# Gathering and combining tokens for one expert at a time in a 64-expert mixture layer, with expert 0's down matrix in another pool

## The chip, the cores and the metric

The kernel runs on one core of one Trainium2 chip. The metric is the device time of one execution in microseconds (us). The names of the engines are those of the profile: PE is the matrix engine (TensorE), PEld its weight loads, DVE the vector engine, ACT the scalar engine, POOL GpSimd, and SP the queue that issues the large transfers. NT = 2 is the number of blocks of 128 tokens.

## The reference, cut to what matters

One decoder layer for 256 tokens of 2048 channels: a mixer, an output projection with a residual, a norm, and then a mixture of 64 experts of width 256, from which each token takes two, and a final norm. The change touches the mixture only.

```python
def hier_moe(x, w_group, b_group, w_router, b_router, w_gate, w_up, w_down):
    """Top-1 expert group, then top-2 experts within that group; SwiGLU experts."""
...
    out = jnp.zeros_like(xt)
    for g in range(N_GROUPS):
        h = jax.nn.silu(jnp.einsum('td,edf->tef', xt, wg[g])) * jnp.einsum('td,edf->tef', xt, wu[g])
        out = out + jnp.einsum('tef,efd->td', h * combine[:, g, :, None], wd[g])
```

All weights are float32. An expert has three matrices of 2 MB: gate (g), up (u) and down (d); below, d5 is the down matrix of expert 5.

## The kernel before

The mixer, the output projection and the routing take the time up to about 381 us. From there the kernel goes through the 64 experts in order. For each it needs a compact copy of the tokens that chose it (32 places, `SLOTS`), the expert's three matrices, and a place to add the result.

**Gather.** `gather(b)` does this for a batch of four experts (`EB`): one comparison makes a 0/1 matrix of 256 tokens by 4 x 32 places (tile `mo`), and 32 matrix products on the full array (`pxg`, L706) pick the tokens, already transposed, in four groups; DVE multiplies each group by the norm's gains into `XT` (L709). The gather of the next batch is called after the second expert of a batch.

**Expert.** `expert` multiplies gate and up (`pgu`, L757) on four column groups of the array, so that four channel blocks are in the PSUM tile under each other. ACT copies the tile (`gs`, L761), eight small products add the four blocks and transpose them (`pgt`, L766), ACT and DVE make silu(gate) * up (L770, L774), and `py` (L783) multiplies with the down matrix, again on four column groups.

**Combine.** The outputs of four experts are copied into four `Y` tiles, and `combine` multiplies them with the transposed combine weights of the batch (`poc`, L722, made by `places`) in 8 products on the full array, each added to the residual `h` by DVE (L805). The last four experts are combined alone: `combine_one` puts one 32-row strip on each of four row groups (L813), and DVE adds (L816).

**Loads.** `loads` issues one transfer for each matrix on SP, in order. Their homes are a ring of 8 tiles of 2 MB in four pools (`rings`), so the load of a matrix waits until PE has read the matrix eight places earlier in the ring. One matrix lies outside the ring: the down matrix of expert 1 goes into the two 8 KB-per-partition tiles (`half_acc`) that hold the residual later; the residual is put there by ACT (L1080) at expert 2. The pool `u8` has three tiles of 8 KB per partition: `mo` and two batches of `XT`.

**The rest.** `overflow` (tokens beyond 32 places, a branch that is not taken here) stands after expert 31. `gains` spreads the final norm's gains (`pgf`, L937) at expert 60. The last expert adds its output into the final norm's pass (`plast`). Tile framework and engine queues run each engine in program order, as placed by the scheduler.

Of the kernel before, what the change touches and what calls it, by code (L numbers as in the profile page):

```python
# [8 lines left out]
F32 = mybir.dt.float32  # L9
# [29 lines left out]
def hymba_kernel(ctx: ExitStack, tc, x, xt, norm_mix_g, w_in, w_gk, gla_norm_g, swa_sinks, w_out, norm_ffn_g, ffn_g_route, w_route,  # L39
# [649 lines left out]
    mo = u8([P, 2, 4, 256], "mo")  # L689
    hn = [0]  # L690

    XT, OC, Y4 = {}, {}, {}


    def gather(b):
        w4 = mo[:, b % 2].rearrange("p a b -> p (a b)")
        oh = w4[:, 0:NT * P].rearrange("p (t e s) -> p t e s", t=NT, e=EB)
        e0 = b * EB
        V.tensor_tensor(oh, iosl[:, None, None, :].to_broadcast([P, NT, EB, SLOTS]),  # L699
                        pos[:, :, e0:e0 + EB, None].to_broadcast([P, NT, EB, SLOTS]), op=OP.is_equal)  # L700
        XT[b] = u8([P, KT, P], f"XT{b}")
        for kg in range(4):
            p = ptmp(f"pxg{b}_{kg}")
            for j in range(4):
                for t in range(NT):
                    TE.matmul(p[:, j * P:(j + 1) * P], hgp[:, t, kg * 4 + j, :],  # L706
                              oh[:, t].rearrange("p e s -> p (e s)"), start=(t == 0), stop=(t == NT - 1))
            k4 = slice(kg * 4, kg * 4 + 4)
            V.tensor_tensor(XT[b][:, k4, :], p.rearrange("p (k i) -> p k i", k=4),  # L709
                            gT[:, k4, None].to_broadcast([P, 4, P]), op=OP.mult)  # L710
            yield


    def places(half, e0, n=EB):
        w4 = mo[:, half % 2].rearrange("p a b -> p (a b)")
        oc = w4[:, 256:256 + NT * P].rearrange("p (t e s) -> p t e s", t=NT, e=EB)
        V.tensor_tensor(oc, iosl[:, None, None, :].to_broadcast([P, NT, EB, SLOTS]),
                        pos[:, :, e0:e0 + n, None].to_broadcast([P, NT, EB, SLOTS]), op=OP.is_equal)
        V.tensor_tensor(oc, oc, Cs[:, :, e0:e0 + n, None].to_broadcast([P, NT, EB, SLOTS]), op=OP.mult)
        p = ptmp(f"poc{e0}")  # L720
# [437 lines left out]
```

## Time and profile before

| what | value |
|---|---|
| time, 3 runs | 1317.43 us median (1314.42 to 1317.8) |
| the profiled execution | 1319.65 us, span 1317.9 us |
| mean granted TensorE clock | 0.922 |
| PE busy | 1119.5 us (85%) |
| DVE busy | 482.9 us (37%) |
| ACT busy | 338.3 us (26%) |
| moved from HBM | 462.70 MB |

The span is the time from the first to the last instruction of the profiled execution; 1.75 us of its time lie outside. Each share is an average over stages: the mixture begins at about 381 us. A granted clock of 1 is full speed (2.4 GHz), of 0.5 half (1.2 GHz). The columns of a timeline row are start, duration, engine, line, operation, result and operands, shape, count and, in brackets, the engine's idle time before it and what ended it.

### The profile page before, as it was taken

The numbers are of one execution on the slowest core, as the hardware profiler recorded it, in microseconds if no ns is written. First come the engines' busy times: TensorE is split into PE (matmuls) and PEld (weight loads), VectorE is DVE, ScalarE is ACT, GpSimd is POOL, SyncE is SP. The second block draws the span as 40 slices with busy tenths as digits, with TensorE's granted clock in tenths as the row PEclk, the third lists the DMA queues.
The fourth block names the chain that finished last, engine by engine and source line by source line (L and its number), as shares of the span: only waits on it lengthen the run. The fifth ranks groups of instructions, "written<-read, shape, count | busy, mean of one in ns | idle before, by whom it ended". The sixth has DMA issues, their size and how long they took to land. (4 is left out here: it accounts for less than half of the span.)

```text
span 1317.9 us, 20950 instructions
## 1 busy us (share of the span) xinstructions
PE 1119.5 (85%) x9167; PEld 713.3 (54%) x9167; DVE 482.9 (37%) x833; ACT 338.3 (26%) x618; POOL 51.9 (4%) x107
## 2 busy tenths in 40 slices
PE   8999999999988987878787887788787787878786
PEld 8988778768875544434353534355353434435332
DVE  5666654455443432222322222223222222323224
ACT  7355554433434111111111111011111111111113
POOL 2120100020100000000000000000000000000002
PEclk9999999999999999888897989799798978889789
DMA  9735335557379999999999999999999999999993
GB/s 348 266 127 192 128 112 195 205 175 273 128 277 429 429 428 429 429 428 430 430 429 429 429 430 419 427 430 430 430 427 429 429 429 430 430 430 430 429 425 151
DMA packets 69391, 466.21 MB, mean 354 GB/s; under 512 B 4700, under 2 KB 25228, under 8 KB 43953
## 3 DMA queue, kind: packets, MB, share of 16 engines
q1 hardware_dynamic: 69058, 464.72, 85.4%
q8 instruction: 73, 1.20, 0.4%
q0 software_dynamic: 240, 0.14, 0.2%
q14 instruction: 20, 0.16, 0.0%
HBM read 462.70 MB, written 2.36 MB: 353 GB/s over the span
## 5 line engine op out<-in xcount | busy, mean ns | idle before, releaser
L757 PE MATMUL pgu<-w,XT 128*32 128x256 f32 x4096 | 266.3, 410 | 77.5 <-DMA w<-in_w_up_dram 47.5
L757 PEld LDWEIGHTS pgu<-w,XT 128*32 128x32 f32 x4096 | 132.9, 117 | 221.9 <-DMA w<-in_w_up_dram 64.1
L783 PE MATMUL py<-w,mo 128*32 128x512 f32 x1008 | 148.7, 715 | 33.5 <-DVE mo L774 17.9
L795 DVE COPY Y<-py 32x512 f32<-32x512 f32 x120 | 82.8, 690 | 191.0 <-ACT Y L797 190.2
L761 ACT ACTIVATE gs<-pgu 128x512 f32<-128x512 f32 x64 | 38.2, 597 | 410.9 <-PE pgu L757 410.7
L774 DVE TENSOR_TENSOR mo<-mo,pgt 128x64 f32<-128x64 f32 x63 | 13.9, 221 | 352.0 <-ACT mo L770 352.0
L803 PE MATMUL pc<-Y,mo 128*128 128x512 f32 x240 | 127.6, 692 | 10.0 <-ACT Y L797 10.0
L797 ACT ACTIVATE Y<-py 32x512 f32<-32x512 f32 x120 | 70.4, 587 | 253.4 <-PE py L783 208.3
L706 PEld LDWEIGHTS pxg<-mo,hgp 128*128 128x128 f32 x1024 | 118.2, 194 | 14.4 <-issue 14.4
L706 PE MATMUL pxg<-mo,hgp 128*128 128x128 f32 x1024 | 124.0, 280 | 0.9 <-DVE mo L699 0.9
L766 PE MATMUL pgt<-id,gs 128*128 128x32 f32 x512 | 73.4, 289 | 48.2 <-ACT gs L761 48.2
L766 PEld LDWEIGHTS pgt<-id,gs 128*128 128x128 f32 x512 | 66.1, 202 | 81.8 <-ACT gs L761 81.8
L803 PEld LDWEIGHTS pc<-Y,mo 128*128 128x128 f32 x240 | 51.8, 224 | 95.3 <-issue 50.3
L805 DVE TENSOR_TENSOR h<-h,pc 128x512 f32<-128x512 f32 x120 | 81.6, 687 | 35.8 <-PE pc L803 35.6
L783 PEld LDWEIGHTS py<-w,mo 128*32 128x32 f32 x1008 | 30.3, 119 | 87.8 <-issue 45.5
L709 DVE TENSOR_TENSOR XT<-pxg,gT 128x512 f32<-128x512 f32 x64 | 44.2, 692 | 60.4 <-PE pxg L706 60.3
L982 POOL IOTA fin<- 128x4 f32 x1 | 0.2, 158 | 899.5 <-DMA w<-in_w_up_dram 899.5
L770 ACT ACTIVATE mo<-pgt 128x64 f32<-128x64 f32 x64 | 14.3, 223 | 78.2 <-PE pgt L766 78.2
L154 PE MATMUL pt<-xh,wi0s 128*128 128x256 f32 x120 | 23.1, 287 | 1.8 <-ACT wi0s L148 1.1
L129 PE MATMUL pjr<-wir_0s,xh 128*128 128x512 f32 x64 | 21.5, 416 | 0.0
L154 PEld LDWEIGHTS pt<-xh,wi0s 128*128 128x128 f32 x120 | 19.0, 191 | 2.5 <-ACT wi0s L148 1.3
L129 PE MATMUL pjr<-wir_1s,xh 128*128 128x512 f32 x64 | 19.9, 391 | 0.0
(392 smaller groups left out, 1395.1 us busy)
## 6 DMA issues: line engine op xcount, KB each, us to landing
w<-in_w_up_dram SPq DMA_DIRECT2D x63, 2048.0 KB, 33.5
w<-in_w_gate_dram SPq DMA_DIRECT2D x63, 2048.0 KB, 34.1
w<-in_w_down_dram SPq DMA_DIRECT2D x62, 2048.0 KB, 32.9
wo<-in_w_out_dram SPq DMA_DIRECT2D x14, 1024.0 KB, 7.2
wt<-in_w_in_dram SPq DMA_DIRECT2D x10, 1024.0 KB, 7.4
wir<-in_w_in_dram SPq DMA_DIRECT2D x8, 1024.0 KB, 7.0
wiv<-in_w_in_dram SPq DMA_DIRECT2D x8, 1024.0 KB, 7.0
wigk<-in_w_in_dram SPq DMA_DIRECT2D x4, 1024.0 KB, 7.1
```

The lines of the kernel that those rows point to most:

```text
L129: TE.matmul(pt, a, w, start=first and i == 0, stop=last and i == 2)
L154: TE.matmul(pt[j], a, v[:, k0 + k, :], start=k0 + k == 0 and i == 0, stop=k0 + k == KT - 1 and i == 2)
L706: TE.matmul(p[:, j * P:(j + 1) * P], hgp[:, t, kg * 4 + j, :], oh[:, t].rearrange("p e s -> p (e s)"), start=(t == 0), stop=(t == NT - 1))
L709: V.tensor_tensor(XT[b][:, k4, :], p.rearrange("p (k i) -> p k i", k=4), gT[:, k4, None].to_broadcast([P, 4, P]), op=OP.mult)
L757: pe[0] = TE.matmul(gu[j * 32:(j + 1) * 32, xw * DE:(xw + 1) * DE], XTe(4 * i + j), w[4 * i + j], start=(i == 0), stop=(i == 3), tile_posi ...
L761: A.activation(gs, gu.rearrange("q (x p f) -> q x f p", x=2, f=2), AF.Copy)
L766: m = TE.matmul(pt[:, c:c + SLOTS], gs[:, xw, f, :], id4, start=True, stop=True)
L783: TE.matmul(y[j * 32:(j + 1) * 32, :], hs[:, f, :], wd[f][:, j * 512:(j + 1) * 512], start=(f == 0 and not last), stop=(f == 1), tile_posi ...
L795: V.tensor_copy(d, y[j * 32:(j + 1) * 32, :])
L797: A.activation(d, y[j * 32:(j + 1) * 32, :], AF.Copy)
L803: TE.matmul(p, oc[:, t, :], y4[cc], start=True, stop=True)
L805: V.tensor_add(a, a, p)
```

## The change

Every expert now gathers its own 32 places. `gather_rows` lets the array hold the 0/1 matrix and stream the activations, on four column groups (8 products `pxg`), which gives token rows; ACT and DVE copy them, four transpositions (`pxt`) turn them, and DVE multiplies by the gains into a small `XT` in pool `t2`. `places` makes the combine weights of one expert, four times side by side, and every expert is combined by what was `combine_one` (now `combine`). Its `Y` and `XT` lie in the six tiles of `t2`. Experts 0 and 1 are combined together with expert 2, since the residual's tiles come free there. The two `u8` tiles that held `XT` take the down matrix of expert 0, so two matrices lie outside the ring of 8.

```diff
-    mo = u8([P, 2, 4, 256], "mo")
+    mo = u8([P, 2, 1024], "mo")
...
+    def gather_rows(oh, n):
+        p = ptmp("pxg" + n)
+        for t in range(NT):
+            for g in range(4):
+                TE.matmul(p[g * 32:(g + 1) * 32, :], oh[:, t], hgp[:, t, 4 * g:4 * g + 4, :].rearrange("p k i -> p (k i)"),
+                          start=(t == 0), stop=(t == NT - 1), tile_position=(0, g * 32))
+        xg = t2([P, 4, P], "xg")
+        x2 = xg.rearrange("p k i -> p (k i)")
+        A.activation(x2[:, 0:256], p[:, 0:256], AF.Copy)
+        V.tensor_copy(x2[:, 256:512], p[:, 256:512])
+        p = ptmp("pxt" + n)
+        for k in range(4):
+            TE.transpose(p[:, k * P:(k + 1) * P], xg[:, k], ident)
+        x = t2([P, 4, 4, SLOTS], "XT")
+        V.tensor_tensor(x, p.rearrange("p (k g s) -> p k g s", k=4, g=4),
...
+    def places(e):
...
+        for t in range(NT):
+            V.tensor_scalar(oc[:, t], iosl[:, None, :].to_broadcast([P, 4, SLOTS]), pos[:, t, e:e + 1], Cs[:, t, e:e + 1],
+                            op0=OP.is_equal, op1=OP.mult)
...
+            elif n == "0" and k == 2:
+                h = [u8([P, DE * KT // k], f"w{len(ws)}{i}_{n}") for i in range(2)]
+                for i in range(2):
+                    SP.dma_start(h[i], rows[:, i])
+                ws.append(h)
...
+        if mid:
+            mid()
...
-        for j in range(4):
-            d = y4[j][slot * 32:(slot + 1) * 32, :]
...
+        yq = t2([P, 512], "Y")
+        A.activation(yq[:, 0:256], y[:, 0:256], AF.Copy)
+        V.tensor_copy(yq[:, 256:512], y[:, 256:512])
+        return yq
...
-        if s == 1:
-            for _ in gather(b + 1):
-                pass
-        if s == 2:
-            places(b, b * EB)
-        if s == EB - 1:
-            combine(Y4[b], OC[b * EB], str(b))
...
+        Y[e] = expert(XT[e], *w, str(e), mid=(lambda: places(e)) if e else None)
         if e == 0:
             Cs = weights()
+            places(0)
+        gather(e + 1)
         if e == 2:
             for t in range(NT):
                 acc[t] = half_acc([P, D], f"h{t}")
                 A.activation(acc[t].rearrange("t (p k) -> t k p", k=KT), hgp[:, t], AF.Copy, scale=rms[:, t:t + 1])
+            combined(Y[0], OC[0], "0")
+            combined(Y[1], OC[1], "1")
+        if 2 <= e < E2:
+            combined(Y[e], OC[e], str(e))
```

Three places in the order of the instructions follow; the names are those of tiles, with the expert's number behind (`w0`, `w1`, `w2` are gate, up and down, `w20` and `w21` the two halves of a down matrix outside the ring).

On SP, the first weight loads before the change, from the last loads of the output projection on:

```order
L745 DMA w1_1_3419<-in_w_up_dram 128x4096
...
L745 DMA w0_2_3522<-in_w_gate_dram 128x4096
...
L745 DMA w1_2_3524<-in_w_up_dram 128x4096
...
L745 DMA w0_0_3308<-in_w_gate_dram 128x4096
L745 DMA w1_0_3310<-in_w_up_dram 128x4096
L745 DMA w2_0_3312<-in_w_down_dram 128x4096
L745 DMA w0_1_3417<-in_w_gate_dram 128x4096
L737 DMA w20_1_3421<-in_w_down_dram 128x2048
L737 DMA w21_1_3422<-in_w_down_dram 128x2048
L745 DMA w2_2_3526<-in_w_down_dram 128x4096
L745 DMA w0_3_3593<-in_w_gate_dram 128x4096
L745 DMA w1_3_3595<-in_w_up_dram 128x4096
L745 DMA w2_3_3597<-in_w_down_dram 128x4096
```

The same place of the changed kernel:

```order
L763 DMA w0_2_3506<-in_w_gate_dram 128x4096
...
L763 DMA w1_2_3508<-in_w_up_dram 128x4096
...
L763 DMA w2_2_3510<-in_w_down_dram 128x4096
...
L763 DMA w0_0_3312<-in_w_gate_dram 128x4096
L763 DMA w1_0_3314<-in_w_up_dram 128x4096
L763 DMA w0_1_3418<-in_w_gate_dram 128x4096
L763 DMA w1_1_3420<-in_w_up_dram 128x4096
L750 DMA w20_1_3422<-in_w_down_dram 128x2048
L755 DMA w20_0_3316<-in_w_down_dram 128x2048
L755 DMA w21_0_3317<-in_w_down_dram 128x2048
L750 DMA w21_1_3423<-in_w_down_dram 128x2048
L763 DMA w0_3_3668<-in_w_gate_dram 128x4096
L763 DMA w1_3_3670<-in_w_up_dram 128x4096
```

The three matrices of expert 2 now go between the output projection's loads, expert 0's down matrix goes in two halves outside the ring, and the gate of expert 3 takes the ring's eighth place, which nothing used before in the mixture; before, it was the ninth in the ring.

On PE, the end of expert 2 before the change (after it the gate of expert 3 follows at once):

```order
L766 MATMUL pgt2_3563<-id4_3277,gs_3561 128x32 x4
L722 MATMUL poc0_3589<-ident_91,mo_3291 128x128 x2
L783 MATMUL py2_3570<-w2_2_3526,mo_3291 32x512 x8
L757 MATMUL pgu3_3599<-w0_3_3593,XT0_3293 32x256 x16
L757 MATMUL pgu3_3599<-w1_3_3595,XT0_3293 32x256 x16
```

and of the changed kernel:

```order
L786 MATMUL pgt2_3553<-id4_3277,gs_3551 128x32 x4
L701 MATMUL pxg3_3573<-hgp_2704,mo_3291 32x512
L803 MATMUL py2_3560<-w2_2_3510,mo_3291 32x512 x8
L701 MATMUL pxg3_3573<-hgp_2704,mo_3291 32x512 x7
L819 MATMUL pc0_00_3596<-Y_3371,mo_3291 128x512
L709 MATMUL pxt3_3585<-ident_91,xg_3582 128x128 x4
L819 MATMUL pc0_10_3597<-Y_3371,mo_3291 128x512
...
L819 MATMUL pc2_00_3644<-Y_3569,mo_3291 128x512
...
L819 MATMUL pc2_31_3659<-Y_3569,mo_3291 128x512
L775 MATMUL pgu3_3674<-w0_3_3668,XT_3590 32x256 x16
```

The gather of expert 3 and the 24 products that combine experts 0, 1 and 2 now stand ahead of the gate of expert 3.

On PE, expert 20 and what follows it before the change:

```order
L757 MATMUL pgu20_4993<-w0_20_4987,XT5_4790 32x256 x16
L757 MATMUL pgu20_4993<-w1_20_4989,XT5_4790 32x256 x16
L766 MATMUL pgt20_5028<-id4_3277,gs_5026 128x32 x4
L783 MATMUL py20_5035<-w2_20_4991,mo_3291 32x512 x8
L757 MATMUL pgu21_5054<-w0_21_5048,XT5_4790 32x256 x16
L757 MATMUL pgu21_5054<-w1_21_5050,XT5_4790 32x256 x16
L766 MATMUL pgt21_5089<-id4_3277,gs_5087 128x32 x4
L706 MATMUL pxg6_0_5111<-mo_3291,hgp_2704 128x128 x8
L706 MATMUL pxg6_1_5121<-mo_3291,hgp_2704 128x128 x8
L783 MATMUL py21_5096<-w2_21_5052,mo_3291 32x512 x8
L706 MATMUL pxg6_2_5131<-mo_3291,hgp_2704 128x128 x8
```

and of the changed kernel:

```order
L775 MATMUL pgu20_5569<-w0_20_5563,XT_5537 32x256 x16
L725 MATMUL poc20_5604<-ident_91,mo_3291 128x128 x2
L775 MATMUL pgu20_5569<-w1_20_5565,XT_5537 32x256 x16
L786 MATMUL pgt20_5610<-id4_3277,gs_5608 128x32 x4
L701 MATMUL pxg21_5630<-hgp_2704,mo_3291 32x512 x8
L803 MATMUL py20_5617<-w2_20_5567,mo_3291 32x512 x8
L709 MATMUL pxt21_5642<-ident_91,xg_5639 128x128 x2
L819 MATMUL pc20_00_5649<-Y_5626,mo_3291 128x512
L709 MATMUL pxt21_5642<-ident_91,xg_5639 128x128 x2
L819 MATMUL pc20_10_5650<-Y_5626,mo_3291 128x512
...
L819 MATMUL pc20_31_5664<-Y_5626,mo_3291 128x512
L775 MATMUL pgu21_5679<-w0_21_5673,XT_5647 32x256 x16
```

Between two gates there now stand a gather, four transpositions and a combine for every expert, and the transposed combine weights between gate and up. Before, the gather of four experts stood around `py` of the second of a batch, and the combine behind its fourth.

## Rows read from the trace of the kernel before

**Rows 1.** Busy time by stretch: stretch, length, engines' busy us, granted clock, DMA share, GB/s.

```profile
376.00:386.00 10.00, 9.02 (x83) 8.49 (x83) 7.00 (x34) 5.48 (x5) 0.57 (x1) 1.00 0.98 398
386.00:392.00 6.00, 5.79 (x64) 4.35 (x64) 2.07 (x4) 0.00 (x0) 0.00 (x0) 1.00 0.08 36
...
400.00:1285.00 885.00, 715.53 (x6618) 385.76 (x6606) 246.03 (x433) 136.94 (x266) 2.89 (x9) 0.89 1.01 429
```

**Rows 2.** Timeline of SP's issues: the loads g3 and d5.

```profile
392.21 0.33 SPq L745 DMA_DIRECT2D w<-in_w_gate_dram  x1
...
422.56 0.33 SPq L745 DMA_DIRECT2D w<-in_w_down_dram  x1
```

**Rows 3.** Issues by time, us to landing last: g3, d5, second half of d63.

```profile
w<-in_w_gate_dram SPq DMA_DIRECT2D x1, 2048.0 KB, 7.7
...
w<-in_w_down_dram SPq DMA_DIRECT2D x1, 2048.0 KB, 17.1
...
w<-in_w_down_dram SPq DMA_DIRECT2D x1, 1024.0 KB, 22.4
```

**Rows 4.** Timeline of the first gather, all engines.

```profile
381.24 0.76 DVE L699 TENSOR_TENSOR mo<-iosl,pos 128x256 f32<-128x256 f32 x2
...
381.82 3.81 PE L706 MATMUL pxg<-mo,hgp 128*128 128x128 f32 x32 [0.94 <-DVE mo L699]
...
383.88 0.69 DVE L709 TENSOR_TENSOR XT<-pxg,gT 128x512 f32<-128x512 f32 x1 [0.47 <-PE pxg L706]
```

**Rows 5.** Timeline of experts 60 to 62, combined alone, all engines.

```profile
1265.82 1.92 PE L783 MATMUL py<-w,mo 128*32 128x512 f32 x16 [0.57 <-DVE mo L774]
...
1267.87 0.38 ACT L789 ACTIVATE Y<-py 128x256 f32<-128x256 f32 x1 [2.36 <-PE py L783]
1268.29 0.42 DVE L790 COPY Y<-py 128x256 f32<-128x256 f32 x1 [2.52 <-ACT Y L789]
...
1268.77 2.00 PE L813 MATMUL pc<-Y,mo 32*128 32x512 f32 x16 [1.02 <-DVE Y L790]
...
1269.93 4.87 DVE L816 TENSOR_TENSOR h<-h,pc 128x512 f32<-128x512 f32 x8 [1.21 <-PE pc L813]
...
1271.87 0.44 PE L722 MATMUL poc<-ident,mo 128*128 128x128 f32 x2 [1.10 <-DVE h L816]
...
1272.23 3.66 PE L757 MATMUL pgu<-w,XT 128*32 128x256 f32 x64
...
1275.96 0.60 ACT L761 ACTIVATE gs<-pgu 128x512 f32<-128x512 f32 x1 [3.24 <-PE pgu L757]
...
1276.61 1.08 PE L766 MATMUL pgt<-id,gs 128*128 128x32 f32 x8 [0.72 <-ACT gs L761]
...
1282.24 3.74 PE L813 MATMUL pc<-Y,mo 32*128 32x512 f32 x16 [1.00 <-DVE Y L790]
```

**Rows 6.** Timeline of ACT at expert 1.

```profile
405.42 3.83 ACT L1080 ACTIVATE h<-hgp,rms 128x2048 f32<-128x2048 f32 x1 [1.60 <-PE py L783]
```

**Rows 7.** Timeline of PE where `py` meets the gather.

```profile
454.65 1.92 PE L783 MATMUL py<-w,mo 128*32 128x512 f32 x16
456.51 4.29 PE L706 MATMUL pxg<-mo,hgp 128*128 128x128 f32 x36
```

**Rows 8.** Timeline of PE: gains, and gate and down of expert 63.

```profile
1252.77 4.94 PE L937 MATMUL pgf<-gfn,one 1*128 1x512 f32 x8
...
1297.15 1.07 PE L757 MATMUL pgu<-w,XT 128*32 128x256 f32 x16
...
1306.67 1.92 PE L783 MATMUL plast<-w,mo 128*32 128x512 f32 x16 [0.83 <-DVE mo L774]
```

**Rows 9.** Timeline of the tail: the last instruction.

```profile
1313.75 1.14 POOL L1039 DMA_INDIRECT out_dram<-fin  x1 [3.06 <-DMA out_dram<-h]
```

**Rows 10.** The page's 40 equal slices: PE busy and granted clock, in tenths.

```profile
PE   8999999999988987878787887788787787878786
...
PEclk9999999999999999888897989799798978889789
```

More of the change, by code (lines that the diff above doesn't have):

```diff
@@ L714, in places @@
[L714 to L720, printed above, removed]
-        for t in range(NT):
-            TE.transpose(p[:, t * P:(t + 1) * P], oc[:, t].rearrange("p e s -> p (e s)"), ident)
-        OC[e0] = w4[:, 512:768].rearrange("p (t i) -> p t i", t=NT)
-        A.activation(OC[e0], p[:, :T].rearrange("p (t i) -> p t i", t=NT), AF.Copy)
+    XT, OC = {}, {}
@@ new lines, in gather, with places_of @@
+    def gather(e):
+        oh = mo[:, e % 2, 0:NT * SLOTS].rearrange("p (t s) -> p t s", t=NT)
+        V.tensor_tensor(oh, iosl[:, None, :].to_broadcast([P, NT, SLOTS]),
+                        pos[:, :, e:e + 1].to_broadcast([P, NT, SLOTS]), op=OP.is_equal)
+        XT[e] = gather_rows(oh, str(e))
+    def places_of(oc, home, n):
+        p = ptmp("poc" + n)
+        for t in range(NT):
+            TE.transpose(p[:, t * P:(t + 1) * P], oc[:, t].rearrange("p j s -> p (j s)"), ident)
+        A.activation(home, p[:, :T].rearrange("p (t i) -> p t i", t=NT), AF.Copy)
+        return home
@@ L749, in hymba_kernel, with expert @@
     pe, ad = [None], [None]
-    def expert(XTe, wg, wu, wd, y4, slot, n, rest=iter(()), last=None, yq=None):
+    def expert(XTe, wg, wu, wd, n, rest=iter(()), last=None, mid=None):
         gu = pacc("pgu" + n)
@@ L786, in expert, with combine @@
             return
[L787 to L808 removed]
+        yq = t2([P, 512], "Y")
+        A.activation(yq[:, 0:256], y[:, 0:256], AF.Copy)
+        V.tensor_copy(yq[:, 256:512], y[:, 256:512])
+        return yq
+    def combine(yq, oc, n, after=None):
         for t in range(NT):
@@ L819, in combine_one, with combined @@
             yield
-    def xslice(b, s):
-        return lambda k: XT[b][:, k, s * SLOTS:(s + 1) * SLOTS]
-    first = gather(0)
-    next(first)
+    def combined(*a):
+        for _ in combine(*a):
+            pass
+    gather(0)
     def weights():
@@ L899, in overflow @@
                 oh = rt.tile([P, NT, SLOTS], F32, name="ooh", bufs=2)
-                oc = rt.tile([P, NT, SLOTS], F32, name="ooc", bufs=2)
+                oc = t2([P, 2, NT, P], "ooc")
                 for t in range(NT):
@@ L1041, in last_out @@
                              in_=o, in_offset=None, bounds_check=4 * T - 1, oob_is_err=False)
[L1044 to L1045 removed]
+    E2, E1 = NE - 2, NE - 1
+    Y = {}
     for e in range(NE):
[L1047 to L1069 removed]
+        if e == E2 - 2:
+            gains()
+        w = w1 if e == E1 else loads(e, str(e))
+        if e == E2:
+            w1 = loads(E1, str(E1))
+            f = raw([P, 2, 4, 512], "fin", rings[nth[0] % len(rings)])
+            for i in range(2):
+                fin["a", i] = f[:, i]
+            last_slots()
+            last_gains()
+        if e == E1:
+            one = combine(Y[E2], OC[E2], str(E2), normed)
+            expert(XT[e], *w, str(e), last_rest(one), last)
+            last_out()
             continue
[L1071 to L1074 removed]
+        Y[e] = expert(XT[e], *w, str(e), mid=(lambda: places(e)) if e else None)
         if e == 0:
             Cs = weights()
+            places(0)
+        gather(e + 1)
         if e == 2:
```

102 lines of the change are left out of this document (17 added, 85 removed).

## The prediction

> **What bounds the kernel now.** I read the table of stretches first [rows 1]. From 400 to 1285 us the DMA is busy all the time (share 1.01, 429 GB/s) while PE works 715.53 of 885 us, DVE 246 and ACT 137. Two MB (2.097 MB) at 429 GB/s take 4.89 us, so an expert's three matrices take 14.7 us: the weight stream is the bound in the experts. Only a late start of the stream, a break in it, or what comes after its last byte can change the time, as long as PE needs less than 14.7 us per expert.
>
> The start: the stream moves 398 GB/s until 386 us and almost nothing (36 GB/s) from 386 to 392 [rows 1]. It waits for a free tile: g3 is issued at 392.21, when PE has read g0 [rows 2], and lands 7.7 us later, at 399.9 [rows 3]; that is the price of a transfer into an empty queue, 2.8 us above the 4.89 of a queued one. From there it does not break: d5, issued at 422.56 [rows 2], lands 17.1 us later [rows 3], at 439.7. These are eight matrices in 39.8 us, 0.7 more than 8 x 4.89.
>
> The end: the second half of d63 is issued at 1274.6 and lands after 22.4 us [rows 3], at 1297.0. From d5 to there are 174 matrices in 857.3 us, 4.93 each. At 1297.0 PE should need only d63, but it only now begins the gate of expert 63, at 1297.15 [rows 8]: it lags behind, since the gains' products alone held it for 4.94 us [rows 8]. The last `py` begins at 1306.67 [rows 8]; the span ends at 1317.9, 11.2 us later, with a store behind other stores [rows 9]. So 20.9 us lie between last byte and end.
>
> The sum below is made against the span of 1317.9 us. The profiled execution's own time, 1319.65, is 1.75 above its span and 2.2 above the median of 1317.43, so the median stands 0.5 below a span worked out in this way. A measurement of this kernel can tell about 0.3% (4 us) from no change.
>
> **The change, part by part.**
>
> *An earlier start.* With d0 outside the ring, g3 is queued without a wait. The queue ran dry at about 386.5, so g3 lands at 391.4 to 393; I take 392.5. The next two reuse g0 and u0. The first gather is one of 8 products of the kind of a `py` (1.92 [rows 5]) in place of 32 around the first gate. From the comparison at 381.24 [rows 4]: comparison about 0.5, gather 1.9, two copies of 0.38 and 0.42 [rows 5], four transpositions 0.9 (two `poc` take 0.44 [rows 5]), gains 0.69 [rows 4]: the gate starts at about 386.1 and frees g0 at 388, u0 at 389.8 (3.66 for both [rows 5]). The queue is still busy, so u3 and d3 land at 397.4 and 402.3. Before, d3 landed at 399.9 + 9.8 = 409.7: **7.3 us gained**.
>
> *The stream breaks again in experts 0 to 2.* Each expert's gate now waits for its own gather, which stands behind the `py` of the expert before.
> - Expert 0: gate and up end at 389.8; copy and transposition (0.72 and 1.08 [rows 5]) and the gap of 0.57 bring `py` to 392.2 to 394.2. The combine weights are made here too (PE to 396), the gather of expert 1 follows (to 398.3), then copies, transpositions and gains: gate 1 at 401.2, g1 free at 403.1, and g4, which reuses it, finds an empty queue and lands at 410.8. Queued it would have landed at 407.2: 3.6 lost.
> - Expert 1: `py` ends at 407.2. ACT begins the residual of 3.83 us [rows 6] as soon as its inputs are there, and `Y` and the copy of the gather are behind it on ACT: gate 2 at 415.4, g2 free and d4 issued at 417.3, landing at 425.0 where 410.8 + 9.8 = 420.6 would have been: 4.4 lost.
> - Expert 2: `py` ends at 423.4, and now 24 products combine three experts ahead of gate 3. DVE adds each in 0.61 (4.87 for eight [rows 5]), the first 1.16 after the products' start [rows 5]. Gate 3's PSUM tile is free after the 17th add: from 425 that is 425 + 1.2 + 17 x 0.61 + 0.69 for the gains of the gather = 437.2. Who waits for that is g3's tile, free at 439.1, and on SP behind it everything: d5 lands at 447.0 where 425.0 + 14.7 = 439.7 would have been: 7.3 lost.
>
> The sum of breaks is 15.3, the gain 7.3; before's own 0.7 above the pure rate is not repeated. d5 lands 15.3 - 7.3 - 0.7 = **7.3 us later** than before (447.0 for 439.7). Bounds: if ACT takes `Y` first and the adds don't hold gate 3, only the first break stands (3.6), and d5 lands 4.4 earlier; if PE also falls to half clock in these experts, at most 5 us more. I take +1.5 for the clock, +0.4 for a short break at d7 (it reuses g5) and +0.5 at the branch after expert 31, where SP stops with one load ahead instead of two: **+9.7 at the last byte, which then lands at 1306.7**.
>
> *The steady expert.* PE's chain from one gate to the next, from rows at full clock [rows 5]: gate and up 3.66, `poc` 0.44, wait for the copy 0.72, `pgt` 1.08, gather 1.92 (it covers the 0.57 for silu), `py` 1.92, wait for `Y` 1.02 (it covers two transpositions), two more transpositions 0.44, combine 2.00. This is 13.2 us. The array's layout changes about six times more often: `py` starts at 454.65 and the full-array gather at 456.51 [rows 7], 1.86 later for 1.92 of its own work, so a change is hidden or nearly so; I take 0.1 each, 0.6 together. 13.8 is under 14.7, so the stream stays the bound, with 0.9 us of slack. The slack of 0.9 would be used up at 0.25 each. The Trainium skill says, on its page "TensorEngine Tiling (Array Packing)", in the section Key Properties, that a change of tiling mode drains TensorE. By that rule nine layouts per expert would cost more than I take; the trace does not show a loss of that size [rows 7].
>
> What is removed (32 full-array products, eight combining products and eight adds per batch, half of the copies of `py`) lay beside the stream and gives nothing there. What is added on DVE, eight adds for each expert in place of eight for four, is 4.87 of 14.7 us; ACT's copies stay under 3 us per expert. Both have room.
>
> *The tail.* The four experts' combine at the end of a batch and the batched gather are gone, and the gains' 4.94 us (half of that at full clock) come into a chain with 0.9 us of slack per expert, three experts before the end. PE should be within about 1 us of the stream. Gate and up of expert 63 are then done before d63 lands, its `py` follows 0.6 to 1.6 us after, and the end 11.2 later: 12.8 from last byte to end in place of 20.9, **8.1 us gained**. Bounds: nothing if the lag stays, 9.1 if none is left.
>
> Sum: 1317.9 + 9.7 - 8.1 = 1319.5 as a span, **1319.0 us** as a median.
>
> **The rivals.**
> - *A: the stream stays the bound, breaks and tail cancel* (above). Its own range is 1312 to 1326: the breaks can be 5 smaller or the clock 5 worse.
> - *B: faster, the early gathers are quick enough.* If ACT and DVE let `Y` and the gains pass ahead of the residual and of the adds, 3.6 of the 15.3 us remain; the last byte lands 9.7 - 11.7 = 2.0 earlier than before, and the tail's 8.1 come on top: 1317.4 - 2.0 - 8.1 = 1307 as a median, and about 1302 without the first break and the 2.4 taken for clock, d7 and branch. For it: such orders are the scheduler's choice. Against it: the 24 products stand ahead of gate 3 on PE itself, and [rows 6] has the residual on ACT ahead of that expert's later copies already.
> - *C: slower, PE becomes the bound.* The point is 14.7 us per expert. At half clock the same combine takes 3.74 in place of 2.00 [rows 5], and the mean grant in the experts is 0.89 [rows 1], which is 22% of the time at half. If that stays, 3.2 us of each expert run at half speed and cost 1.6: 13.8 + 1.6 = 15.4, and 60 times 0.7 is 42 us: about 1355, less if only half the experts are hit (1335). Against it: the page's slices [rows 10] show the clock at 9 wherever PE is at 9 and the falls where PE is at 7 or 8, that is, where it waits for weights; a PE that lags doesn't wait, and gets its clock back.
> - *D: slower, the adds hold the matrix engine.* The page "TensorEngine Tiling (Array Packing)" of the Trainium skill, section PSUM Bottleneck, warns that tiling speeds up TensorE but not the emptying of PSUM. As a mechanism here: a combine has 2.00 us of products and 4.87 of adds [rows 5], so 2.9 us of waiting for each expert if gate and up of the next had to wait: 13.8 + 2.9 = 16.7, 60 x 2.0 = 120 us more, 1437. Against it: eight products go to eight PSUM tiles, and what follows, gate and up, takes one of them, whose add is long done. In [rows 5] `poc` did wait 1.10 for an add, and gate 62 followed at once.
>
> **How the numbers follow.** A 0.57, B 0.18, C 0.21, D 0.04. Within A, 0.41 lie within 4 us of the median, 0.03 below, 0.13 above. So faster 0.21, same 0.41, slower 0.38. The range runs from 1302, B's lower end, to 1350, which leaves out D and about half of C (0.14), and takes in the slow bound of the early experts.
>
> **What will show each step right or wrong.** The gather of expert 0 should let the gate begin at about 386, and g3 should not wait. The DMA share from 400 to 450 us should fall in three places, the longest ending when the load of d5 is issued at about 439. From 460 on it should be 1.0 again, with a PE that waits for weights each 14.7 us and a clock at least at 0.89. From last byte to end about 13 us. The prediction is wrong if PE's waits for weights vanish and the distance of two gates goes over 15 us (C, D), or if the 24 products don't delay gate 3 (B).

## The result and the profile after

The changed kernel takes 1344.91 us (median of 6 runs, 1342.99 to 1346.26) against 1316.71 for the kernel before in the same runs: 1.0217 times as long, 95% interval 1.0204 to 1.023. That is 28 us slower, where no change was forecast (1319), inside the range of 1302 to 1350. The profiled executions, whose rows follow, lie closer together: the one before took 1319.65 and the changed one 1342.99, 23.3 apart.

The stretches that answer to [rows 1], and the early and late ones apart (columns as there):

```profile
386.00:392.00 6.00, 4.57 (x71) 2.38 (x68) 1.34 (x3) 0.39 (x2) 0.00 (x0) 1.00 1.02 427
...
400.00:1285.00 885.00, 799.77 (x7554) 357.49 (x7546) 442.06 (x909) 120.94 (x304) 0.00 (x0) 0.96 0.98 413
...
400.00:454.00 54.00, 47.73 (x394) 23.39 (x386) 22.25 (x47) 13.19 (x18) 0.00 (x0) 0.91 0.70 277
454.00:482.00 28.00, 24.25 (x220) 11.99 (x219) 16.52 (x37) 2.74 (x7) 0.00 (x0) 0.88 0.93 368
482.00:830.00 348.00, 322.68 (x3120) 146.42 (x3123) 182.66 (x372) 45.81 (x124) 0.00 (x0) 0.98 1.01 428
830.00:880.00 50.00, 41.97 (x376) 17.55 (x372) 22.02 (x46) 5.51 (x15) 0.00 (x0) 0.86 0.85 356
880.00:1257.00 377.00, 337.78 (x3247) 147.49 (x3240) 186.68 (x386) 48.46 (x130) 0.00 (x0) 0.97 1.01 429
```

The stream no longer stops from 386 to 392. Against 429 GB/s it loses 19 us of the 54 from 400 on (277), 4 of the next 28 (368) and 8.5 of the 50 from 830 on (356), and next to nothing elsewhere. PE is busy 84 us longer between 400 and 1285 (799.77 for 715.53), at a clock of 0.96 for 0.89.

SP's issues that answer to [rows 2], and the two around the branch:

```profile
379.43 0.65 SPq L763 DMA_DIRECT2D w<-in_w_gate_dram  x1
390.20 0.33 SPq L763 DMA_DIRECT2D w<-in_w_up_dram  x1
...
405.71 0.33 SPq L763 DMA_DIRECT2D w<-in_w_gate_dram  x1
...
445.70 0.33 SPq L763 DMA_DIRECT2D w<-in_w_down_dram  x1
...
815.35 0.33 SPq L763 DMA_DIRECT2D w<-in_w_down_dram  x1
846.03 0.33 SPq L763 DMA_DIRECT2D w<-in_w_gate_dram  x1
```

g3 is issued at 379.43, d5 only at 445.70 (422.56 before), and between 815 and 846 us SP issues nothing. The loads that answer to [rows 3], g3, d5 and the second half of d63, which is issued at 1298.1:

```profile
w<-in_w_gate_dram SPq DMA_DIRECT2D x1, 2048.0 KB, 16.4
...
w<-in_w_down_dram SPq DMA_DIRECT2D x1, 2048.0 KB, 8.1
...
w<-in_w_down_dram SPq DMA_DIRECT2D x1, 1024.0 KB, 25.4
```

So g3 lands at 395.8, d5 into an empty queue at 453.8 (439.7 before), and the last byte at 1323.5, 26.5 us later than before (the 14.1 of d5, 4.0 behind it and 8.5 at the branch); from there to the end of the span (1341.3) it takes 17.8 in place of 20.9.

What PE waited for between 480 and 1090 us (waits by engine, in total, times, longest):

```profile
PE pgt L786 <- ACT gs L781: 26.2, 43, 0.8
PE pxt L709 <- ACT xg L705: 23.5, 30, 0.9
PE poc L725 <- DVEq L884: 2.8, 1, 2.8
PE pgu L775 <- DMA w<-in_w_up_dram: 0.7, 1, 0.7
```

PE waits 0.7 us for weights in 610 us. **PE is the bound now**, over 40 experts, although the stream runs at 428 to 429 GB/s beside it outside the break at the branch: it runs into the eight places of the ring and gets them as PE frees them. The two waits that come most often are for copies by ACT, of `gs` and of the gathered rows `xg`.

Why does the stream not fall below its rate then? Two timelines of PE, expert 10 and expert 20, show how near the two are:

```profile
542.93 3.66 PE L775 MATMUL pgu<-w,XT 128*32 128x256 f32 x64
...
547.31 1.08 PE L786 MATMUL pgt<-id,gs 128*128 128x32 f32 x8 [0.35 <-ACT gs L781]
548.32 1.05 PE L701 MATMUL pxg<-hgp,mo 128*32 128x512 f32 x2
548.97 2.12 PE L803 MATMUL py<-w,mo 128*32 128x512 f32 x16
550.71 1.89 PE L701 MATMUL pxg<-hgp,mo 128*32 128x512 f32 x14
552.53 1.12 PE L819 MATMUL pc<-Y,mo 32*128 32x512 f32 x2
...
556.09 1.28 PE L775 MATMUL pgu<-w,XT 128*32 128x256 f32 x19
```

```profile
680.93 1.93 PE L775 MATMUL pgu<-w,XT 128*32 128x256 f32 x32
...
685.82 1.08 PE L786 MATMUL pgt<-id,gs 128*128 128x32 f32 x8 [0.72 <-ACT gs L781]
686.82 1.92 PE L701 MATMUL pxg<-hgp,mo 128*32 128x512 f32 x16
688.56 1.90 PE L803 MATMUL py<-w,mo 128*32 128x512 f32 x16
691.24 0.44 PE L709 MATMUL pxt<-ident,xg 128*128 128x128 f32 x2 [0.78 <-ACT xg L705]
691.61 1.12 PE L819 MATMUL pc<-Y,mo 32*128 32x512 f32 x2
...
695.16 1.07 PE L775 MATMUL pgu<-w,XT 128*32 128x256 f32 x16
```

From gate to gate expert 10 takes 13.16 us, expert 20 takes 14.23. In expert 10 seven of the eight gather products stand behind `py` and cover the copies of its output; in expert 20 all eight stand ahead of it, and PE waits 0.78 for the copies. In expert 20 `poc` also stands between gate and up, and the wait for `gs` is 0.72 in place of 0.35. From expert 16 on the scheduler chose the second order (again from 35 on, after the branch). With stretches at half clock the mean from expert 35 (904.66) to 48 (1093.96) is 14.56, for 14.7 us of stream: a PE that is late stays late, or nearly so.

The tail answers to [rows 8, 9]:

```profile
1320.54 1.07 PE L775 MATMUL pgu<-w,XT 128*32 128x256 f32 x16
...
1329.76 1.92 PE L803 MATMUL plast<-w,mo 128*32 128x512 f32 x16 [0.83 <-DVE mo L794]
```

```profile
1336.88 1.14 POOL L1034 DMA_INDIRECT out_dram<-fin  x1 [3.10 <-DMA out_dram<-h]
```

Gate 63 starts 23.4 us later than before, and the span ends 23.4 later: the whole loss between the two profiled executions is PE's lateness. Where it arises is seen in the starts of the first gates on PE:

| gate of expert | before | after | PE is late by |
|---|---|---|---|
| 0 | 385.56 | 388.21 | 2.6 |
| 2 | 412.76 | 417.31 | 4.6 |
| 3 | 420.59 | 442.50 | 21.9 |
| 5 | 446.04 | 477.16 | 31.1 |
| 16 | 597.96 | 622.58 | 24.6 |
| 63 | 1297.15 | 1320.54 | 23.4 |

The 2.6 us at gate 0 are largely this execution's own: six kernels below have the same code up to there and begin it at 384.13 to 386.50. The loss is made in experts 2 to 4: the combine of three experts ahead of gate 3, and then the count of overflow tiles, whose second product stops PE in the gate and up of expert 4, before PE goes on at half clock.

```profile
430.23 12.34 PE L819 MATMUL pc<-Y,mo 32*128 32x512 f32 x46
...
462.84 0.20 PE L871 MATMUL pend<-before,moreb 64*128 64x64 bf16 x1 [1.93 <-DVE moreb L866]
```

From gate to gate expert 4 takes 19.5 us, where expert 10 takes 13.16. From gate 5 to gate 16, at 13.16 for most experts, 6.5 of the 31.1 us are made up, and from there to the end 1.2.

### The profile page after: what moved, and what is told of

Its sections match the earlier page's. It is cut to its first block, busy times and chain, and to the rows that moved or that the text cites. A ratio compares the mean times of both kernels' runs of the same rounds, so it can differ in the third digit from the quotient of the medians.

```text
span 1341.3 us, 24066 instructions
## 1 busy us (share of the span) xinstructions
PE 1223.6 (91%) x10233; PEld 689.7 (51%) x10233; DVE 688.9 (51%) x1335; ACT 325.6 (24%) x667; POOL 52.1 (4%) x107
## 5 line engine op out<-in xcount | busy, mean ns | idle before, releaser
L822 DVE TENSOR_TENSOR h<-h,pc 128x512 f32<-128x512 f32 x504 | 312.5, 682 | 67.8 <-PE pc L819 61.8
L819 PE MATMUL pc<-Y,mo 32*128 32x512 f32 x1008 | 223.7, 688 | 0.0
L701 PE MATMUL pxg<-hgp,mo 128*32 128x512 f32 x1024 | 143.8, 600 | 0.7 <-DVE mo L717 0.7
L819 PEld LDWEIGHTS pc<-Y,mo 32*128 32x128 f32 x1008 | 80.4, 193 | 63.4 <-issue 35.5
L810 DVE COPY Y<-py 128x256 f32<-128x256 f32 x63 | 26.8, 425 | 134.8 <-ACT Y L809 134.7
L709 PEld LDWEIGHTS pxt<-ident,xg 128*128 128x128 f32 x256 | 26.1, 141 | 128.4 <-ACT xg L705 93.9
L709 PE MATMUL pxt<-ident,xg 128*128 128x128 f32 x256 | 52.5, 297 | 38.3 <-ACT xg L705 38.2
L701 PEld LDWEIGHTS pxg<-hgp,mo 128*32 128x32 f32 x1024 | 34.8, 110 | 46.2 <-issue 35.4
L733 DVE TENSOR_SCALAR mo<-iosl,pos,Cs 128x128 f32<-128x128 f32 x126 | 37.7, 343 | 18.5 <-PE poc L725 18.3
L711 DVE TENSOR_TENSOR XT<-pxt,gT 128x512 f32<-128x512 f32 x64 | 43.8, 684 | 0.5 <-PE pxt L709 0.5
```

The costliest lines, as they stand in the source:

```text
L701: TE.matmul(p[g * 32:(g + 1) * 32, :], oh[:, t], hgp[:, t, 4 * g:4 * g + 4, :].rearrange("p k i -> p (k i)"), start=(t == 0), stop=(t == N ...
L709: TE.transpose(p[:, k * P:(k + 1) * P], xg[:, k], ident)
L711: V.tensor_tensor(x, p.rearrange("p (k g s) -> p k g s", k=4, g=4), gT.rearrange("p (g k) -> p k g", g=4)[:, :, :, None].to_broadcast([P, ...
L733: V.tensor_scalar(oc[:, t], iosl[:, None, :].to_broadcast([P, 4, SLOTS]), pos[:, t, e:e + 1], Cs[:, t, e:e + 1], op0=OP.is_equal, op1=OP.mult)
L810: V.tensor_copy(yq[:, 256:512], y[:, 256:512])
L819: pe[0] = TE.matmul(p[cc], oc[r, t, :], yq[r, :], start=True, stop=True, tile_position=(cc * 32, 0))
```

## The experiments

All times are medians, with the ratio to the kernel before on the same chip and its 95% interval; the changed kernel stands at 1344.91 and 1.0217. The kernel before has medians of 1315.23 to 1317.79 on the chips used, so that a difference of 2 to 3 us between kernels of different chips tells nothing. Starts of gates are those of the profiled executions.

**Loads of expert 32 ahead of the branch**

```diff
-    Y = {}
+    Y, pre = {}, {}
...
-        w = w1 if e == E1 else loads(e, str(e))
+        w = w1 if e == E1 else pre.pop(e, None) or loads(e, str(e))
...
         if e == NE // 2 - 1:
+            for i in (e + 1,):
+                pre[i] = loads(i, str(i))
             overflow()
```

> The changed kernel with the three loads of expert 32 issued before the branch after expert 31 (the changed kernel lets the gate of expert 33, which waits for the up matrix of expert 31, stand ahead of them). Theory 'the stream sets the end, and its breaks are the loss': the break between 830 and 880 us (356 in place of 429 GB/s in 50 us, 8.5 us) goes, and the time falls by 7 to 8.5 us, to about 1337. Rival 'PE is the bound from expert 16 on': PE waited only 0.7 us for weights there, so at most 1 to 2 us come back, to about 1343.

Measured 1340.39, 1.017 [1.0146, 1.0194]. The break is nearly gone (830 to 880 us: 411 GB/s) and the last byte lands 5.8 us earlier, at 1317.7, but from there to the end it now takes 22.1 us in place of 17.8. The stream's theory is right on the stream; the time lies between its 1337 and the rival's 1343. PE's own lateness moves little: beside the changed kernel, gate 31 starts 0.7 us later and gate 63 1.4 earlier, 2.1 in all.

**Without the combine of experts 0 and 1**

```diff
-            combined(Y[0], OC[0], "0")
-            combined(Y[1], OC[1], "1")
```

> The changed kernel without the combine of experts 0 and 1 (16 products and 16 adds left out, so their part of the output is missing). Theory 'breaks of the stream': gate 3 starts some 10 us earlier, at about 432.5 in place of 442.5, the longest break (10.1 us ahead of the landing of the down matrix of expert 5) goes to nearly nothing, and the time falls by 8 to 10 us, to about 1336. Rival 'the stream catches up anyway, PE sets the end by its work alone': only the 16 products' own 4 us, to about 1341.

Measured 1335.83, 1.0143 [1.0127, 1.016]: 9.1 us less. Gate 3 starts at 430.94 in place of 442.50, straight after the eight products of expert 2:

```profile
429.01 1.99 PE L819 MATMUL pc<-Y,mo 32*128 32x512 f32 x14
430.94 3.66 PE L775 MATMUL pgu<-w,XT 128*32 128x256 f32 x64
```

Of the 11.6 us between the two starts of gate 3, 1.0 are there at gate 2 already, so the 16 products and their adds cost 10.6 us of PE at that place, and most of it arrives at the end: 8.5 at gate 63, 9.1 in the median. That is the stream's theory in its number; the rival's 4 us is ruled out.

**The gains at expert 40**

```diff
-        if e == E2 - 2:
+        if e == 40:
             gains()
```

> The changed kernel with the final norm's gains spread at expert 40 in place of 60, the same instructions elsewhere. Theory 'PE lags behind the stream at the end because of the gains': from last byte to end 13 to 14 in place of 17.8 us, the last byte no later, the time 3 to 5 us lower, about 1341. Rival 'PE is the bound from expert 16 on': the same PE work earlier changes nothing, 1345.

Measured 1340.98, 1.0186 [1.0163, 1.0209]. The size fits, the place does not: the last byte lands 4.2 us earlier (1319.3), and from there to the end it takes 19.5, not less. The 2.6 us that PE waited for weights from 1090 to 1270 (four waits) are gone, but the trace does not show a gain by the move: gate 0 starts 3.4 us earlier than in the changed kernel, gate 39, still ahead of the move, 3.6, and gate 63 2.5. With intervals that overlap, what the move itself is worth stays open.

**d0 back in the ring**

```diff
-            elif n == "0" and k == 2:
-                h = [u8([P, DE * KT // k], f"w{len(ws)}{i}_{n}") for i in range(2)]
-                for i in range(2):
-                    SP.dma_start(h[i], rows[:, i])
-                ws.append(h)
```

> The changed kernel with the down matrix of expert 0 back in the ring, the two tiles of 8 KB left empty. Theory 'the stream waits for the gate of expert 1 anyway': the gate of expert 3 is issued at about 390 and lands at 398 in place of 395.8, the load of the gate of expert 4 is issued at 405.7 as before, and the time stays within 1.5 us of the changed kernel. Rival 'the earlier start is worth what it gains (4 us)': 1349.

Measured 1343.45, 1.0206 [1.0188, 1.0225]: no difference that can be told, as expected. An earlier start of the stream shows no worth where PE is the bound.

**Gather products held behind the down product for all experts**

```diff
+                with tc.issue_after(lastpy[0].ins) if lastpy[0] and n != "o" and (t or g) else nullcontext():
...
-                TE.matmul(y[j * 32:(j + 1) * 32, :], hs[:, f, :], wd[f][:, j * 512:(j + 1) * 512],
+                lastpy[0] = TE.matmul(y[j * 32:(j + 1) * 32, :], hs[:, f, :], wd[f][:, j * 512:(j + 1) * 512],
```

> The changed kernel with seven of the eight gather products of the next expert held behind the down product of this one for all experts (from expert 16 on the scheduler had put all eight ahead of it, and PE then waited 0.8 us for the copies of the output). Theory 'stream and PE are nearly balanced, and a PE of 14.2 to 14.6 us per expert never catches up': the distance of two gates falls from 14.23 to about 13.2 where PE does not wait for weights, the last byte stays at about 1322, from last byte to end 14 in place of 17.8 us: 1341. Rival 'PE alone is the bound': 1 us for each of 45 experts, 1300 to 1310. Rival 'a PE that waits loses its clock again': no change, 1345.

Measured 1332.76, 1.0135 [1.011, 1.0161]: 12 us less, three times what the balance expected and a third of what 'PE alone' expected. From gate to gate it is 13.66 us from expert 16 to 23, not 13.2 (14.23 in the changed kernel). The last byte lands at 1318.2, 5.3 us earlier and not where it was, and 13.3 lie behind it. The late experts:

```profile
890.00:1240.00 350.00, 321.44 (x3062) 141.25 (x3058) 179.42 (x365) 47.53 (x121) 0.00 (x0) 1.00 1.01 429
```

and PE's waits for weights from 480 to 1270 us:

```profile
PE pgu L777 <- DMA w<-in_w_up_dram: 11.2, 28, 1.3
PE py L805 <- DMA w<-in_w_down_dram: 7.5, 28, 0.5
```

PE now waits 18.7 us for weights in place of 0.7 up to 1090 and 2.6 after: the stream is the bound again from about expert 24 to the branch, where gates come every 14.6 us, and from about expert 40 on. The clock did not fall with these short waits, it is 1.00. PE comes to expert 31 earlier, and so even the break at the branch is smaller (408 GB/s from 820 to 880 us, 367 in the changed kernel). The early loss is not smaller (255 GB/s from 400 to 454 us, 277 in the changed kernel); it and the branch are left.

**That order, the loads ahead and the gains at 40**

> That order, the loads of expert 32 ahead of the branch, and the gains at expert 40. Theory of balance: with a PE that keeps up, the break at the branch is worth its whole 8.5 us and the tail 4.5: 1332. Rival 'the parts do not add up': what loads (4.5) and gains (3.9) gave apart, 1336.5 or more.

Measured 1331.81, 1.012 [1.0098, 1.0142]: 1 us below the order alone, which is not a difference. The time is the balance's 1332, but by luck: it was added up from an order worth 4 us, which gave 12, and 13 for the other two, which gave 1 here. That all three mend the same lateness of PE, so that little is left for the others once PE keeps up, is the reading that fits; no run shows it by itself.

**Everything, with the early experts rearranged**

Not shown in the diff: the tile for the outputs, and the count of overflow tiles, which moves to expert 8.

```diff
+    gather(1)
...
-        gather(e + 1)
+        if e < 8:
+            gather(e + 2)
+        elif e > 8:
+            gather(e + 1)
...
-                A.activation(acc[t].rearrange("t (p k) -> t k p", k=KT), hgp[:, t], AF.Copy, scale=rms[:, t:t + 1])
-            combined(Y[0], OC[0], "0")
-            combined(Y[1], OC[1], "1")
+                G.tensor_scalar(acc[t].rearrange("t (p k) -> t k p", k=KT), hgp[:, t], rms[:, t:t + 1], None, op0=OP.mult)
+        for i in {0: (), 1: (), 2: (0,), 3: (1, 2), 4: (3, 4), E2: ()}.get(e, (e,)):
+            combined(Y[i], OC[i], str(i))
```

> The same, and the early experts rearranged: the gather of expert 1 ahead of expert 0 and each gather two experts ahead up to expert 9, the residual set up by POOL in place of ACT, the outputs of experts 0 to 3 kept in a free tile and combined one, two and two at a time after experts 2, 3 and 4, and the overflow's count of tiles moved from expert 3 to 8. Theory 'the early breaks are made by the own gather, the residual on ACT and the 24 products': the stream runs without a break from 390 us on, the down matrix of expert 5 lands at 435 to 438 in place of 453.8, the last byte at about 1295, the end 13 later: 1310 (1306 to 1316), faster than both kernels. Rival 'PE does not have the time for 64 own gathers and combines': no better than 1325.

Measured 1324.56, 1.0072 [1.0055, 1.0089]: 20 us less than the changed kernel, and a miss of 14 against what was expected: by its number it is the rival's side ('no better than 1325'), which the next kernel rules out. The stream still loses 11.7 us from 400 to 454 (336 GB/s). POOL needs 14.13 us for the residual, and while it works some operations of the vector engine stand (last section), so the down product of expert 2 waits 3.12 us for one of them and then runs in part at half clock; two combines each after experts 3 and 4 bring these to 17.8 us from gate to gate.

```profile
408.33 14.13 POOL L1077 TENSOR_SCALAR h<-hgp,rms 128x2048 f32<-128x2048 f32 x2 [32.38 <-PE py L806]
```

**The residual by ACT and the vector engine, the late combines at 6 and 10**

The diff is against the kernel above. Not shown in it: only the outputs of experts 0 and 1 stay in the free tile, and the count of overflow tiles moves on, from expert 8 to 12.

```diff
-                G.tensor_scalar(acc[t].rearrange("t (p k) -> t k p", k=KT), hgp[:, t], rms[:, t:t + 1], None, op0=OP.mult)
+                if t:
+                    V.tensor_scalar(acc[t].rearrange("t (p k) -> t k p", k=KT), hgp[:, t], rms[:, t:t + 1], None, op0=OP.mult)
+                else:
+                    A.activation(acc[t].rearrange("t (p k) -> t k p", k=KT), hgp[:, t], AF.Copy, scale=rms[:, t:t + 1])
-        for i in {0: (), 1: (), 2: (0,), 3: (1, 2), 4: (3, 4), E2: ()}.get(e, (e,)):
+        for i in {0: (), 1: (), 6: (6, 0), 10: (10, 1), E2: ()}.get(e, (e,)):
```

> Like the kernel with everything rearranged (order, loads ahead of the branch, gains at expert 40, gathers two experts ahead), but the residual is set up by ACT and the vector engine in place of POOL, and the combines of experts 0 and 1 wait in a free tile until experts 6 and 10. Theory 'what broke the stream in that kernel was POOL's 14 us for the residual and the two experts with two combines': no expert of the first ten takes PE over 14.7 us but expert 6 and 10, nothing is lost from 400 to 480 us (12 to 16 there), the last byte lands at 1296 to 1299 in place of 1308.8, the end 12.3 later: 1308 to 1312, 5 us or more faster than the kernel before. Rival 'the early experts are short of PE time whatever the order': 1318 or more.

Measured 1311.6, 0.9979 [0.997, 0.9987]. The time is the one expected, and faster than both kernels; the gain over the one before is 3.6 us, less than the 5 that were expected and than the 4 us named as telling, though its interval lies below 1. The last byte lands at 1298.6, the end 12.3 later. Three things changed at once, so their shares are not told apart; and the stream still loses 4.8 us from 400 to 454 (391 GB/s, below), where nothing was expected.

**The same with d0 in the ring**

> The same with the down matrix of expert 0 in the ring. Theory 'its place outside the ring was worth nothing only because the stream broke behind it': now the stream does not break, so the start comes back as a loss, 2 to 4 us slower than the kernel it is made from. Rival: no difference, as in the changed kernel.

Measured 1311.68, 0.9975 [0.9964, 0.9987]: the rival. The stretches of the kernel with d0 outside the ring, and then of this one:

```profile
376.00:400.00 24.00, 21.36 (x180) 11.77 (x183) 10.27 (x46) 9.05 (x12) 0.00 (x0) 0.93 0.92 368
400.00:454.00 54.00, 50.93 (x502) 24.72 (x494) 24.77 (x52) 11.35 (x22) 0.00 (x0) 1.00 0.95 391
```

```profile
376.00:400.00 24.00, 20.10 (x180) 11.23 (x183) 12.49 (x54) 9.50 (x13) 1.64 (x3) 1.00 0.78 303
400.00:454.00 54.00, 50.93 (x508) 24.64 (x504) 23.70 (x50) 11.74 (x23) 0.00 (x0) 1.00 1.00 426
```

What the stream gains before 400 us with d0 outside (368 for 303 GB/s) it loses after 400 (391 for 426): in both PE does the same work in the same time, and the ring's eight places cover a start that is 4 us later.

**The count of overflow tiles at expert 12**

```diff
-        if e == 3:
+        if e == 12:
             span, nmore, turn = tiles()
```

> The changed kernel with the count of overflow tiles at expert 12 in place of 3 (the gate and up of expert 4 wait 5 us for its second product there). Theory 'every wait of PE up to the point where the stream has its eight places ahead breaks the stream': the 4.0 us lost from 454 to 482 us (368 in place of 429 GB/s) go, 1341. Rival 'PE's lag only moves to expert 13, since it never catches up': 1344 to 1345.

Measured 1344.6, 1.0218 [1.0172, 1.0263]: the rival's number, though four runs from 1339.19 to 1350.69 can't tell it from the theory's 1341. The trace decides. The early break goes and the one at the branch grows (367 GB/s in the same 60 us of the changed kernel):

```profile
454.00:482.00 28.00, 27.30 (x268) 13.64 (x270) 16.22 (x33) 3.73 (x10) 0.00 (x0) 1.00 1.01 428
820.00:880.00 60.00, 50.30 (x438) 20.79 (x434) 26.42 (x54) 6.25 (x17) 0.00 (x0) 0.89 0.79 327
```

Gate 4 starts 1.3 us earlier than in the changed kernel, gate 5 7.6 (469.60), so the count cost expert 4 6.3 us. Of these PE stands 1.9 for the second product, not 5 as the expectation has it; the rest is mostly half clock behind it. Expert 13, where the count now stands, pays it in turn, and gate 16 starts at 622.59, where the changed kernel has 622.58. A break of the stream is not itself the loss.

**The gather two experts ahead**

The edit is the gathers' part of the diff of the kernel with everything (`gather(1)` ahead, `gather(e + 2)` up to expert 7).

> The changed kernel with the gather of expert 1 ahead of expert 0 and each gather two experts ahead up to expert 9; the residual on ACT and the 24 products stay. Theory 'the own gather of the next expert behind each down product makes the first two breaks': the loads of the gates of expert 4 and the down matrix of 4 are issued 3 to 5 us earlier, so the down matrix of expert 5, too: 1340. Rival 'only the 24 products count': 1344 to 1345.

Measured 1337.63, 1.0174 [1.0145, 1.0202]: 7.3 us less, more than the theory's 5; the rival is ruled out. Gate 2 starts at 411.1 in place of 417.3; of these 6.2 us 4.2 are left at gate 5, 5.5 at gate 16, and at gate 63 it is 8.2. The load of d5 is issued only 2.4 us earlier (443.30), behind the 24 products: the gain follows PE's lead rather than that load.

**The combine's part of the change alone, in the kernel before**

```diff
-        if b == LB:
-            if s == 0:
+        if b >= 1:
+            if e == NE - 4:
                 gains()
...
+            if s == 1 and b < LB:
+                for _ in gather(b + 1):
+                    pass
```

> The kernel before with one part of the change alone: from expert 4 on every expert is combined alone on row groups, the gather stays one for four experts and all weights stay in the ring. Theory: the stream stays unbroken, the last byte lands at about 1297, PE needs about 13.4 us per expert, the tail is shorter since no batch is combined at expert 59: 1313 to 1317. Rival 'the adds on the vector engine (4.87 us per expert) hold PE, which waits for one ahead of each transposition of the combine weights': over 14.7 us per expert, 1330 or more.

Measured 1375.98, 1.0456 [1.0439, 1.0474], the rival's side, and far beyond its 1330. Two of its experts, without a gather between their products:

```profile
667.45 2.00 PE L813 MATMUL pc<-Y,mo 32*128 32x512 f32 x16 [0.96 <-DVE Y L790]
670.55 0.44 PE L722 MATMUL poc<-ident,mo 128*128 128x128 f32 x2 [1.10 <-DVE h L816]
670.92 3.66 PE L757 MATMUL pgu<-w,XT 128*32 128x256 f32 x64
675.29 1.08 PE L766 MATMUL pgt<-id,gs 128*128 128x32 f32 x8 [0.72 <-ACT gs L761]
676.94 2.83 PE L783 MATMUL py<-w,mo 128*32 128x512 f32 x16 [0.57 <-DVE mo L774]
680.71 3.80 PE L813 MATMUL pc<-Y,mo 32*128 32x512 f32 x16 [0.94 <-DVE Y L790]
```

Each wait of the chain is bare: 0.57, 0.96, 1.10 and 0.72 us in one expert, the third of them for an add (32.7 us in 38 waits from 480 to 1270 us). The granted clock is 0.88 from 890 to 1240 us, and `pc` takes 3.80 in place of 2.00 where it falls. Four experts with their gather take 61.5 us (658.54 to 720.08), 15.4 each. In the changed kernel the own gather stands in the gap ahead of `py`, and in the first order also in the one behind it; `poc` stands beside gate and up and waits for no add, and the clock is 0.96 from 400 to 1285 us. That the gather, which looked like added work, is what fills the gaps and keeps the clock is argued from the two traces: no run adds it alone to this kernel, and this one also stands at the branch (236 GB/s from 820 to 880 us).

## Why the prediction held in its range and failed in its middle

**The steady expert: the step that failed.** The forecast was case A, 'the stream stays the bound', on 13.8 us of PE for 14.7 of stream. At full clock the order of experts 5 to 15 gives 13.16, that of experts 16 on 14.23, and half clock brings that to 14.56. So the slack was 0.1, not 0.9, and a PE that is late stays late. The terms that failed are the wait for `Y` of 1.02, which was said to cover two transpositions, and the combine of 2.00 in one piece. In expert 20 these transpositions wait for a copy on ACT, too, and run only after it, and the first product of the combine stands alone between them: from the first transposition (691.24) to the next gate (695.16) it takes 3.92, where the sum had 0.44 and 2.00; the terms ahead of it came 0.45 shorter.

Rival C had the right bound with another cause. It was to come from half clock at a grant of 0.89, with gates over 15 us apart; the clock rose to 0.96, as the argument against C had it, and gates are 14.2 to 14.6 apart. Its 1355 is not the sum of its terms either: 42 us on the 1317 that D's sum starts from are 1359. What a lost slack costs is not 0.7 for each expert but what PE loses in the first five and can't make up, 23 us in the span. The experiments with the order (12 us back) and with the count of tiles (gate 16 where it was) show it: what PE loses early is lost unless PE is faster than the stream later.

That 1344.91 lies in the range is in good part luck: the range went up to 1350 to take in half of C and the slow bound of the early experts, and A's own ended at 1326. By the terms of the forecast the span came 21.8 us above its 1319.5: about 6.8 at d5, 2.1 from there to 482 us (where 1.5 for the clock and 0.4 for d7 stood), 8.0 at the branch and 5.0 in the tail. These are places where a late PE shows, rather than four causes: with the break at the branch nearly gone the median fell by 4.5, not 8.

**The early experts.** The mechanism held, step by step: d5 is held by 24 products, the residual's 3.78 stands on ACT ahead of `Y`, g4 and d4 find empty queues. The sizes were short. The three breaks were put at 3.6, 4.4 and 7.3 and came as 3.4, 5.4 and 10.1, since gate 2 began 1.9 us later than forecast and PE ran parts of the gates of experts 2 and 3 at half clock (5.35 and 4.86 us in place of 3.66); so the load of d5 was put at 439.1 and came at 445.70. The start gained 4.2 us, not 7.3 (the first comparison came 2.5 us later, g3 landed at 395.8 and d3 at 405.5). Not in the sum: the count of overflow tiles, which costs expert 4 6.3 us.

**The branch.** 0.5 us was put there; the stream loses 8.5. On SP the gate of expert 33, which waits for the up matrix of 31, stands ahead of the branch, and the loads of 32, whose places come free before, behind it. With those loads ahead of the branch the kernel's median is 4.5 us lower, of which the trace shows 2.1 on PE.

**The tail.** 17.8 us, not 12.8: of the 8.1 to be gained 3.1 came. The last `py` begins 6.3 us after the last byte (9.7 before), where 0.6 to 1.6 was forecast: PE keeps most of its lag, near the bound of 'nothing if the lag stays'.

**The layouts and the adds.** The 0.6 us for changes of layout can't be told from these rows. Expert 10 has six changes and takes 13.16 us, close to the 13.2 of the sum, but by luck: its only wait is 0.35, where the sum had 0.72 and 1.02, and its combine, in two pieces around the transpositions, takes 1.05 and 1.92 to the start of what follows, where one piece takes 2.00 in [rows 5]. Whether the change of layout costs this 1 us, or a product that stands alone, no run here separates. The Trainium skill's rule on the page "TensorEngine Tiling (Array Packing)", section Key Properties, is that a change of mode drains TensorE. The page gives no price, and this case neither shows a cost of 0.6 us nor excludes it. The mechanism of rival D, adds that hold PE, is not in the changed kernel's waits above, and is in the kernel that has the combine alone, with 32.7 us in 790. The Trainium skill warns in the section PSUM Bottleneck of the same page that the copy out of PSUM may become the bottleneck after tiling. The two traces bear it out only where what follows on PE needs the tile of a late add.

## What to carry to other kernels

A stream that is busy all the time does not show that it is the bound: look at whether the engine that frees its buffers ever waits for it. Where the two need nearly the same time, lateness is hardly made up (31.1 us at gate 5, 23.4 at gate 63 here), and most of what the first few rounds lose is paid at the end. Cost a chain of short waits in the order in which the scheduler issues it, copy by copy; work that stands in its gaps may cost less than it seems.

## What the runs showed of the hardware

Setting up 128x2048 of the residual takes 7.07 and 7.14 us on POOL (14.13 for two), 3.77 to 3.83 on ACT and 2.00 on the vector engine. While POOL did it, from 408.33 to 422.46, two small operations of the vector engine took 5.40 us in place of 0.60, and ended as POOL ended:

```profile
404.78 0.60 DVE L736 TENSOR_SCALAR mo<-iosl,pos,Cs 128x128 f32<-128x128 f32 x2 [2.72 <-PE poc L728]
...
410.53 2.39 DVE L720 TENSOR_TENSOR mo<-iosl,pos 128x64 f32<-128x64 f32 x1 [0.65 <-PE pxg L704]
...
417.20 5.40 DVE L736 TENSOR_SCALAR mo<-iosl,pos,Cs 128x128 f32<-128x128 f32 x2 [2.73 <-PE poc L728]
```

The Trainium skill has this on its page "SBUF — State Buffer", section Who interferes with whom: the vector engine and GpSimd share a pair of ports as an exclusive lock, and the later one waits. The trace agrees for this pair of operations. A comparison beside POOL's first operation took 2.39 us in place of 0.23 and ended 2.5 us ahead of it, and copies out of PSUM and the gains took their usual 0.41 to 0.69 beside it: not every operation stood.

The granted clock was 1.00 from 890 to 1240 us in the kernel with the order held, where PE waited 59 times, 28.3 us in all and 35 times for weights. In the same 350 us it was 0.88 in the kernel with the combine alone, where PE waited 90 times, 68.1 us in all.
